# Weight parts made by two transfers and a ScalarE negation instead of a ScalarE copy and a VectorE subtraction

## The chip, the core and the metric

The kernel runs on one core of a Trainium2 chip. The metric is the device time of one execution in microseconds (us). The engines are named as the profile names them: PE is TensorE's matmuls, PEld its weight loads, DVE VectorE, ACT ScalarE, POOL GpSimd, SP the SyncE queue, which issues nearly every transfer of the kernel before.

## What is computed

The reference is one inference step of a two-layer network over 640 tokens (128 of context, 512 latent), with 1024 features, in float32. Each layer normalises its input, projects it with `w_in`, runs three token mixers beside each other (differential attention, a state-space scan, neighbourhood attention), merges them through gates, and projects with `w_out`:

```
def _pre(x, cvec, norm_g, w_ada, b_ada, w_in):
    ada = (jax.nn.silu(cvec) @ w_ada + b_ada)[..., None, :]
    shift, scale, gate = jnp.split(ada, 3, axis=-1)
    hmod = _rmsnorm(x, norm_g) * (1.0 + scale) + shift
    parts = jnp.split(hmod @ w_in, np.cumsum(IN_SIZES)[:-1].tolist(), axis=-1)
    return parts, gate

def _post(x, gate, ya, ga, yb, yc, gc, merge_logits, w_br_a, w_br_b, w_br_c, w_out):
    ma, mb, mc = jnp.split(jax.nn.sigmoid(merge_logits), N_BRANCH, axis=-1)
    merged = (ma * ((ya * jax.nn.silu(ga)) @ w_br_a) + mb * (yb @ w_br_b)
              + mc * ((yc * jax.nn.silu(gc)) @ w_br_c))
    return x + gate * (merged @ w_out)
```

The last layer is followed by one more normalisation. The matrices that the change touches are `w_in` (in the kernel `w_feat`, `w_v` and `w_z`, cut by use), the three `w_br` and `w_out`. `w_ada` goes another way.

## The kernel before, in words

**Exact pairs.** A float32 matrix product is made of three products in the type float32r, which keeps fewer bits. Every operand is held as a pair: `hi`, the value rounded to float32r, and `lo`, the rest. `feat` (L156) and `tok` (L173) multiply high by high, high by low and low by high into one PSUM bank. So each weight block must be in SBUF as two tiles before PE can use it: `lo` is wanted by the third product after the first use of `hi`.

**Where the pairs come from.** `weights` (L136) makes the pair of one block, a "set" in what follows. It is called 194 times: 12 sets of 256 KB (128 x 512) at the very start, 182 of 512 KB (8 of them 528 KB). SP loads the block into `raw`; ACT copies it into `hi`, which rounds (L144); DVE subtracts `hi` from `raw` into `lo` (L145). There are two `raw` tiles, three `hi` and three `lo`. A `raw` tile is free as soon as DVE has read it, so the next loads run while PE is still busy with older sets. A `hi` and a `lo` tile are free when PE has made its last product with them. The two `raw` tiles also take the blocks of `w_ada` that `ada_part` loads during neighbourhood attention.

**What a set feeds.** Most sets feed 48 products of 320 columns (`feat`, both halves of the tokens). The 12 sets at the start and the 32 of `w_out` feed 24 each, since `out_proj` loads each block once for each half of the tokens. `w_z` and `w_v` (8 sets each over both layers) are used two sets at a time by `tok`: five token tiles, each with 12 products of the first set and then 12 of the second.

**Order of the stages.** A start that loads x and the first adaLN blocks and works on the 12 small sets; then per layer the state-space branch with `w_z`, `w_v` and logits; differential attention; neighbourhood attention; and the tail, `merges` of the third branch and `out_proj` for each half. A scheduler in the framework sets the order of the instructions on each engine from the program and its own model of durations. At run time each engine takes its instructions strictly in that order, and each waits at its place. A transfer that POOL issues stands in POOL's order like its arithmetic. POOL in the kernel before makes products for the rotary embedding (L392) and the scan (L690, L735, L757), small powers for the norms (L191, L294) and fills padding (L573); it issues no transfer.

Of the kernel before, what the change touches and what calls it, by code (L numbers as in the profile page):

```python
# [19 lines left out]
EPS = 1e-6  # L20
# [11 lines left out]
# what fills the waits of each head (pair): logits of branches a and c, merges of branch a; and what stands before it  # L32
# [86 lines left out]
class Net:  # L119
# [15 lines left out]
    # ---- weights, each as an exact pair of float32r parts  # L135
    def weights(self, src, k, n):  # L136
        """[128, k, n] from DRAM -> its two parts."""
        nc = self.nc
        view = lambda t: t[:, 0:k * n].rearrange("p (k n) -> p k n", k=k)
        raw = view(self.wraw.tile([128, 1056], F32, tag="raw", name="raw"))  # L140
        self.dma(raw, src)
        hi = view(self.whi.tile([128, 1056], F32R, tag="hi", name="hi"))
        lo = view(self.wlo.tile([128, 1056], F32R, tag="lo", name="lo"))
        nc.scalar.activation(hi, raw, AF.Copy)  # L144
        nc.vector.tensor_tensor(out=lo, in0=raw, in1=hi, op=ALU.subtract)  # L145
        next(self.side, None)
        return hi, lo
# [10 lines left out]
    def feat(self, w, rhs, evac, m=0, halves=(0, 1), part=None):  # L158
        """128 output features of 640 tokens, handed to evac(half, PSUM [128, 320]); part: of a half of the rows alone."""
# [13 lines left out]
    def tok(self, w, t, n):  # L173
        """[128 tokens, n] of a token tile in PSUM."""
# [10 lines left out]
    def rstd(self, pool, ps, scale, n, eps_scale=1.0):  # L185
        """(ps * scale + EPS) ** -0.5 for a narrow [128, n]."""
# [12 lines left out]
    # ---- constants  # L199
# [33 lines left out]
    # ---- adaLN vectors: [128, feature tiles, 2 (context, latent)] each  # L233
    def ada_part(self, src, bias, dst, raws, p, pp):
        """1024 columns, side by side over the four column groups of the PE array; one step per 128 rows."""
# [18 lines left out]
    def ada(self, l, out, raws, p, pp):  # L254
        """Shift and scale, as (shift, (1 + scale) * norm_g) of four feature tiles each."""
# [20 lines left out]
    # ---- RMS of x over features, for one half of the tokens: PSUM [128, 320] of 1/rms on every partition  # L276
# [44 lines left out]
    def gate_in(self, l, c, p):  # L321
        """2 * silu of a gate tile."""
# [17 lines left out]
    # ---- differential attention  # L340
# [36 lines left out]
    def lat_part(self, half):  # L377
        """Where the latents of a half lie: in PSUM, among the latents."""
        return (slice(128, 320), slice(0, 192)) if half == 0 else (slice(0, 320), slice(192, 512))
# [43 lines left out]
    def diff_attn(self, l, h, v, kq, nlam, p, cp, ps, pp, after_ctx):  # L423
        """The head's output times the first map's normaliser, and that normaliser per token."""
# [8 lines left out]
        def soft(s, n, t):  # L433
            """exp(scale * (s - max)) of both maps, s [128, 2, n]; the first plus c times the second."""
# [15 lines left out]
        # context queries read context keys alone  # L450
# [13 lines left out]
        for qp in range(2):  # L464
            ph = p.tile([128, 6, 256], F32R, tag="ph", name="ph")
            pl = p.tile([128, 6, 256], F32R, tag="pl", name="pl")
            for qi in range(2):
# [12 lines left out]
                # the low parts of both maps side by side, each on its half of the rows and in its own bank  # L480
# [22 lines left out]
    def diff_norm(self, att, cp, pp):  # L503
        """Normaliser of the head's features per token, spread over the diagonals of a [128, 640]."""
# [13 lines left out]
        # rows of both parts of r, one token tile each  # L518
# [22 lines left out]
    # ---- state-space branch  # L541
    def ssd(self, l):
        nc, a, o, sm = self.nc, self.a, self.o, self.sm
        with ExitStack() as es:
# [97 lines left out]
            # softplus: max(x, 0) + log1p(exp(-|x|)), log1p(e) = 2 atanh(e / (2 + e))  # L642
# [26 lines left out]
            # decays: to the chunk's end (0, 1), from its start (2, 3), over all of it (4, 5); per direction  # L669
# [120 lines left out]
    # ---- neighbourhood attention: keys by blocks of eight columns (7, 0, 1, ..., 6), queries by tiles of sixteen columns  # L790
    def na_vkq(self, l, hp, p, pp, after_v=lambda: None):
# [17 lines left out]
        # values, token-major through transposes  # L809
# [26 lines left out]
        # keys  # L836
# [17 lines left out]
        # queries  # L854
# [22 lines left out]
    def na_ctx(self, vkq, y, p, ps, pp):  # L877
        """Context queries read context keys alone."""
# [77 lines left out]
    # ---- gated merge of one branch: twice its term, summed in DRAM or handed out  # L956
# [208 lines left out]
```

## Time and profile before

| | |
|---|---|
| median of the runs | 1662.32 us (2 runs, 1660.53 to 1664.1) |
| profiled execution, span | 1666.2 us |
| PE busy | 1601.4 us, 96% |
| DVE busy | 1062.0 us, 64% |
| ACT busy | 769.3 us, 46% |
| POOL busy | 149.8 us, 9% |
| transfers | 214.61 MB, 129 GB/s in the mean |

Matmuls are pipelined: each is shown for some 0.31 us, though one follows another every 0.14 us, so a busy PE can still be waiting a little. The page has the sums over the span; the trace behind it can be asked for one stretch, one engine or one line. In a row of the trace "idle before <-releaser" tells how long the engine stood still before the instruction and what ended that.

### The profile page before, as it was taken

The page shows a single profiled execution, that of the slowest core. Times are in us where ns is not written, and L with a number is a line of the kernel's source. Part 1 is how long each engine was busy: PE and PEld are TensorE (multiplying, and loading weights), DVE is VectorE, ACT ScalarE, POOL GpSimd, SP SyncE. Part 2 cuts the span into 40 slices and gives each one's busy share as a digit, 9 for nine tenths or more (in the row PEclk, how much of TensorE's full clock was granted, in tenths as well). Part 3 has the DMA queues.
Part 4 walks back from the last instruction along what each step waited for, and adds up shares of the span by engine and source line. Part 5 has one row for each costly group of instructions (what it writes and reads, how often), then busy time and mean ns, then how long its engine had stood idle before and what let it go on. Part 6 is the DMA issues. An engine that isn't in the chain of part 4 may idle for free.

```text
span 1666.2 us, 28800 instructions
## 1 busy us (share of the span) xinstructions
PE 1601.4 (96%) x11166; PEld 1495.2 (90%) x11166; DVE 1062.0 (64%) x2287; ACT 769.3 (46%) x1776; POOL 149.8 (9%) x170
## 2 busy tenths in 40 slices
PE   4999999999999999999999999999999999999997
PEld 2998898999888888889989989988998898999997
DVE  3886767657546465566688668756565374667566
ACT  3647633345444454443446565334444354554432
POOL 0005210101000000000000242201010000000000
PEclk9999999999999999999999999999999999999998
DMA  9422235322265755457542222352222946445553
GB/s 300 125 87 74 83 125 157 96 79 78 75 123 147 155 133 156 152 189 264 175 129 85 83 87 87 115 184 69 72 84 73 161 143 118 111 126 164 192 168 132
DMA packets 114824, 214.61 MB, mean 129 GB/s; under 512 B 36736, under 2 KB 52608, under 8 KB 114688
## 3 DMA queue, kind: packets, MB, share of 16 engines
q1 hardware_dynamic: 114688, 212.78, 44.2%
q8 instruction: 88, 1.44, 0.4%
q14 instruction: 48, 0.39, 0.1%
HBM read 170.27 MB, written 34.08 MB: 123 GB/s over the span
## 4 chain that ended last, share of the span: by engine, by line
PE 74%; DMA 12%; DVE 6%; ACT 3%; issue 3%; SPq 1%; POOL 1%; POOLq 0%; DVEq 0%; ACTq 0%
PE mm L170 51%; PE mm L182 7%; DMA raw<-in_w_feat 4%; DVE lo L145 2%; PE s L913 2%; PE t L929 1%; ACT hi L144 1%; DMA qd<-qr 1%; PE o L498 1%; PE o L937 1%; DMA aw<-in_w_ada 1%; PE g L740 1%; PE ada L242 1%; PE y L753 1%; PE t L490 1%
## 5 line engine op out<-in xcount | busy, mean ns | idle before, releaser
L170 PE MATMUL mm<-hh,hi 128*128 128x320 f32 x1856 | 581.0, 313 | 6.0 <-ACT hh L317 4.4
L170 PE MATMUL mm<-hl,hi 128*128 128x320 f32 x1856 | 580.4, 313 | 2.4 <-DVE hl L318 2.4
L170 PE MATMUL mm<-hh,lo 128*128 128x320 f32 x1856 | 576.7, 311 | 0.5 <-DVE lo L145 0.5
L170 PEld LDWEIGHTS mm<-hh,hi 128*128 128x128 f32 x1856 | 350.7, 189 | 25.8 <-issue 13.1
L170 PEld LDWEIGHTS mm<-hl,hi 128*128 128x128 f32 x1856 | 350.8, 189 | 10.4 <-issue 4.5
L170 PEld LDWEIGHTS mm<-hh,lo 128*128 128x128 f32 x1856 | 351.3, 189 | 6.3 <-issue 4.3
L145 DVE TENSOR_TENSOR lo<-raw,hi 128x1024 fp32r<-128x1024 f32 (+2 forms) x194 | 235.4, 1214 | 158.1 <-ACT hi L144 157.4
L144 ACT ACTIVATE hi<-raw 128x1024 fp32r<-128x1024 f32 (+2 forms) x194 | 200.0, 1032 | 246.7 <-PE mm L170 127.0
L170 PE MATMUL mm<-yh,hi 128*128 128x320 f32 x384 | 121.6, 318 | 8.8 <-DVE th L981 7.1
L170 PE MATMUL mm<-yl,hi 128*128 128x320 f32 x384 | 120.1, 313 | 0.2 <-DVE yl L338 0.2
L170 PE MATMUL mm<-yh,lo 128*128 128x320 f32 x384 | 119.3, 311 | 0.0
L182 PE MATMUL mm<-lo,hh 128*128 128x264 f32 (+1 forms) x320 | 90.7, 284 | 0.0
L182 PE MATMUL mm<-hi,hl 128*128 128x264 f32 (+1 forms) x320 | 90.7, 284 | 0.0
L182 PE MATMUL mm<-hi,hh 128*128 128x264 f32 (+1 forms) x320 | 90.2, 284 | 0.0
L170 PEld LDWEIGHTS mm<-yh,hi 128*128 128x128 f32 x384 | 72.7, 190 | 15.2 <-DVE th L981 9.3
L492 ACT ACTIVATE ph<-t 128x384 fp32r<-128x384 f32 x64 | 31.3, 489 | 113.3 <-PE t L490 113.3
L437 DVE TENSOR_REDUCE st<-s 128x2 f32<-128x1536 f32 (+1 forms) x40 | 59.5, 1487 | 30.4 <-PE s L483 25.8
L170 PE MATMUL mm<-mgh,lo 128*128 128x320 f32 x256 | 78.3, 308 | 0.4 <-DVE lo L145 0.4
L170 PE MATMUL mm<-mgl,hi 128*128 128x320 f32 x256 | 78.6, 308 | 0.0
L170 PE MATMUL mm<-mgh,hi 128*128 128x320 f32 x256 | 77.5, 306 | 0.0
L170 PEld LDWEIGHTS mm<-yl,hi 128*128 128x128 f32 x384 | 73.1, 190 | 0.6 <-DVE yl L338 0.4
L170 PEld LDWEIGHTS mm<-yh,lo 128*128 128x128 f32 x384 | 73.2, 191 | 0.0
(286 smaller groups left out, 2865.7 us busy)
## 6 DMA issues: line engine op xcount, KB each, us to landing
raw<-in_w_feat SPq DMA_DIRECT2D x110, 512.0 KB, 3.7
raw<-in_w_ada SPq DMA_DIRECT2D x32, 512.0 KB, 4.4
raw<-in_w_out SPq DMA_DIRECT2D x32, 512.0 KB, 3.9
thd<-th SPq DMA_DIRECT2D x48, 320.0 KB, 2.2
th<-thd SPq DMA_DIRECT2D x48, 320.0 KB, 3.8
raw<-in_w_br SPq DMA_DIRECT2D x24, 512.0 KB, 3.6
accd<-th SPq DMA_DIRECT2D x32, 320.0 KB, 3.5
ac<-accd SPq DMA_DIRECT2D x32, 320.0 KB, 4.5
```

The source lines that it names most:

```text
L144: nc.scalar.activation(hi, raw, AF.Copy)
L145: nc.vector.tensor_tensor(out=lo, in0=raw, in1=hi, op=ALU.subtract)
L170: nc.tensor.matmul(ps, lhsT=s, rhs=r, start=(k == 0 and n == 0), stop=(k == K - 1 and n == 2))
L182: nc.tensor.matmul(ps, lhsT=s, rhs=r, start=(k == 0 and q == 0), stop=(k == 7 and q == 2))
L242: nc.tensor.matmul(ps[32 * g:32 * g + 32, :], lhsT=self.sc[:, k, :], rhs=raw[:, 256 * g:256 * g + 256], start=(k == 0), stop=(k == 7))
L437: nc.vector.tensor_reduce(out=st[:, 0:2], in_=s, axis=AX.X, op=ALU.max)
L490: nc.tensor.transpose(pt[:, i, :], e[:, kt * 128:(kt + 1) * 128], self.ident)
L492: nc.scalar.activation(ph[dst], pt[:, 0:3, :], AF.Copy)
L498: nc.tensor.matmul(ov[:, 0:256], lhsT=x[:, kt, sv], rhs=q[:, kt, :], start=(kt == 0 and n == 0), stop=(kt == 5 and n == 2))
L740: nc.tensor.matmul(sg, lhsT=self.trir[:, d, :], rhs=rh.rearrange("p h n -> p (h n)"), start=(d == 0 and i == 0), stop=(d == 1 and i == 1))
L753: nc.tensor.matmul(yd[:, h * 64:h * 64 + 64], lhsT=ma[:, r], rhs=xt[:, c, h * 64:h * 64 + 64], start=True, stop=True)
L913: nc.tensor.matmul(s[:, c0:c0 + n], lhsT=q[:, i * 128:(i + 1) * 128], rhs=ks[j][:, k0:k0 + n], start=(x == 0), stop=(x == 1))
```

## The change

`weights` no longer loads `raw`. POOL issues a transfer from DRAM straight into the `hi` tile; since source and destination differ in type, the transfer rounds. ACT writes the negated `hi` into the `lo` tile. POOL then issues a second transfer of the same block into `lo` that adds to what is there. The VectorE subtraction is gone, and so is SP's part. The pools keep their sizes: three `hi`, three `lo`, two `raw`, which now serve `w_ada` alone. Everything else in the diff is removed comments and docstrings; by that, later lines move up by two.

```diff
     def weights(self, src, k, n):
-        """[128, k, n] from DRAM -> its two parts."""
-        nc = self.nc
+
         view = lambda t: t[:, 0:k * n].rearrange("p (k n) -> p k n", k=k)
-        raw = view(self.wraw.tile([128, 1056], F32, tag="raw", name="raw"))
-        self.dma(raw, src)
         hi = view(self.whi.tile([128, 1056], F32R, tag="hi", name="hi"))
         lo = view(self.wlo.tile([128, 1056], F32R, tag="lo", name="lo"))
-        nc.scalar.activation(hi, raw, AF.Copy)
-        nc.vector.tensor_tensor(out=lo, in0=raw, in1=hi, op=ALU.subtract)
+        self.nc.gpsimd.dma_start(out=hi, in_=src)
+        self.nc.scalar.activation(lo, hi, AF.Copy, scale=-1.0)
+        self.nc.gpsimd.dma_start(out=lo, in_=src, accum_op=ALU.add)
         next(self.side, None)
         return hi, lo
```

The order of the instructions changes with it. On POOL, late in the state-space branch of the first layer, where logits follow one another, the kernel before had only its own arithmetic (`rh` and `xw` are scan products, `rs` a power):

```order
L735 TENSOR_TENSOR rh<-masks,lh 128x512 x4
L757 TENSOR_TENSOR ysb<-xt,ds 128x512
L191 TENSOR_TENSOR rs<-rv,mhalf 128x1
L757 TENSOR_TENSOR ysb<-xt,ds 128x512
L191 TENSOR_TENSOR rs<-rv,mhalf 128x1
```

At the same place the change has (numbers tell the sets apart; `lo` is always one more than its `hi`):

```order
L141 DMA hi_2603<-in_w_feat 128x1024
L755 TENSOR_TENSOR ysb_1878<-xt_694,ds_692 128x512
L143 DMA lo_2604<-in_w_feat 128x1024
L141 DMA hi_2662<-in_w_feat 128x1024
L189 TENSOR_TENSOR rs_1896<-rv_1894,mhalf_116 128x1
L143 DMA lo_2663<-in_w_feat 128x1024
L755 TENSOR_TENSOR ysb_1992<-xt_694,ds_692 128x512
L141 DMA hi_2745<-in_w_feat 128x1024
L143 DMA lo_2746<-in_w_feat 128x1024
```

The two transfers of a set stand one behind the other, and the next set's first transfer stands behind the second of the set before; POOL's arithmetic stands between them.

In `out_proj` of the first layer the loads stood on SP, ahead of PE by as many as buffers allowed, mixed with stores of x (`xd`):

```order
L133 DMA raw_8970<-in_w_out 128x1024
L133 DMA raw_9003<-in_w_out 128x1024
L133 DMA xd_105<-x0_8855 128x320
L133 DMA xd_105<-x1_8856 128x320
L133 DMA raw_9036<-in_w_out 128x1024
L133 DMA raw_9069<-in_w_out 128x1024
```

Now they stand on POOL, three sets under way at a time:

```order
L141 DMA hi_8883<-in_w_out 128x1024
L141 DMA hi_8915<-in_w_out 128x1024
L143 DMA lo_8884<-in_w_out 128x1024
L141 DMA hi_8947<-in_w_out 128x1024
L143 DMA lo_8916<-in_w_out 128x1024
L143 DMA lo_8948<-in_w_out 128x1024
L141 DMA hi_8979<-in_w_out 128x1024
```

Here the first transfers of two further sets go ahead of the second transfer of the first one.

On ACT, among the logits of the same stretch as the first pair of fences, the kernel before had the rounding copy, with the evacuations of PSUM (`th`) around it:

```order
L962 ACTIVATE th_2447<-mm_2454 128x320
L144 ACTIVATE hi_2630<-raw_2628 128x1024
L962 ACTIVATE th_2447<-mm_2480 128x320
L743 ACTIVATE ee<-g 128x512
L787 ACTIVATE yh_97<-yf 128x128
```

and the change has the negation, which reads what the first transfer brings:

```order
L960 ACTIVATE th_2425<-mm_2457 128x320
L142 ACTIVATE lo_2604<-hi_2603 128x1024
L960 ACTIVATE th_2484<-mm_2490 128x320
L773 ACTIVATE ysq,yst<-ysb 128x512
L960 ACTIVATE th_2484<-mm_2516 128x320
```

The ACT instruction of a set keeps its place between two evacuations, but what it waits for is now a transfer that could not start before the buffer was free.

## Rows read from the trace of the kernel before

**Rows 1.** The page: span, then busy time of each engine.
```profile
span 1666.2 us, 28800 instructions
PE 1601.4 (96%) x11166; PEld 1495.2 (90%) x11166; DVE 1062.0 (64%) x2287; ACT 769.3 (46%) x1776; POOL 149.8 (9%) x170
```

**Rows 2.** PE's waits: for what, us in total, times, longest.
```profile
PE ada L242 <- DMA aw<-in_w_ada: 16.0, 5, 13.7
PE mm L170 <- DVE th L981: 7.1, 6, 2.8
...
PE mm L170 <- DVE hl L318: 2.4, 2, 1.8
...
PE mm L170 <- DVE lo L145: 1.0, 2, 0.5
```

**Rows 3.** Groups by line: busy us, mean ns | idle before, releasers.
```profile
L145 DVE TENSOR_TENSOR lo<-raw,hi 128x1024 fp32r<-128x1024 f32 (+2 forms) x194 | 235.4, 1214 | 158.1 <-ACT hi L144 157.4
L144 ACT ACTIVATE hi<-raw 128x1024 fp32r<-128x1024 f32 (+2 forms) x194 | 200.0, 1032 | 246.7 <-PE mm L170 127.0 <-DMA raw<-in_w_feat 72.3 <-DMA raw<-in_w_out 28.1
```

**Rows 4.** ACT's timeline among logits: start, us, instruction [idle before <-releaser].
```profile
227.27 1.06 ACT L144 ACTIVATE hi<-raw 128x1024 fp32r<-128x1024 f32 x1 [2.21 <-PE mm L170]
228.23 0.42 ACT L962 ACTIVATE th<-mm 128x320 f32<-128x320 f32 x1
...
234.67 1.06 ACT L144 ACTIVATE hi<-raw 128x1024 fp32r<-128x1024 f32 x1 [1.42 <-PE mm L170]
...
241.60 1.06 ACT L144 ACTIVATE hi<-raw 128x1024 fp32r<-128x1024 f32 x1 [1.29 <-PE mm L170]
```

**Rows 5.** Stretches: bounds, length, busy (count) by engine, PEclk, DMA share, GB/s.
```profile
0.00:45.00 45.00, 23.22 (x176) 11.95 (x177) 19.48 (x60) 15.97 (x37) 2.38 (x18) 0.92 0.91 292
45.00:83.00 38.00, 38.00 (x265) 38.00 (x265) 32.05 (x79) 21.69 (x44) 0.34 (x6) 1.00 0.38 120
500.00:780.00 280.00, 271.45 (x1933) 247.71 (x1932) 160.13 (x401) 125.03 (x318) 2.24 (x13) 1.00 0.59 164
805.00:851.00 46.00, 46.00 (x320) 45.84 (x319) 35.28 (x79) 23.67 (x41) 0.85 (x1) 1.00 0.62 192
1606.00:1653.00 47.00, 46.55 (x321) 46.13 (x320) 31.74 (x57) 17.83 (x26) 0.85 (x1) 1.00 0.47 152
1653.00:1666.20 13.20, 2.75 (x12) 1.50 (x10) 5.61 (x14) 0.47 (x1) 0.85 (x1) 0.61 0.29 99
```

**Rows 6.** ACT's timeline inside `out_proj` of the first layer.
```profile
814.96 1.06 ACT L144 ACTIVATE hi<-raw 128x1024 fp32r<-128x1024 f32 x1 [2.64 <-DMA raw<-in_w_out]
...
817.91 1.06 ACT L144 ACTIVATE hi<-raw 128x1024 fp32r<-128x1024 f32 x1 [1.54 <-DMA raw<-in_w_out]
```

**Rows 7.** ACT's timeline where one pair of `w_z` sets follows another.
```profile
97.16 1.09 ACT L144 ACTIVATE hi<-raw 128x1056 fp32r<-128x1056 f32 x1 [1.12 <-PE mm L182]
98.56 0.39 ACT L638 ACTIVATE sz<-mm 128x256 f32<-128x256 f32 x1 [0.32 <-PE mm L182]
```

**Rows 8.** PE's timeline in the same place: start, us, product.
```profile
96.31 0.28 PE L182 MATMUL mm<-lo,hh 128*128 128x264 f32 x1
96.42 0.28 PE L182 MATMUL mm<-hi,hl 128*128 128x264 f32 x1
```

**Rows 9.** Transfers: count, KB each, median us from issue to landing.
```profile
raw<-in_w_feat SPq DMA_DIRECT2D x110, 512.0 KB, 3.7
...
raw<-in_w_feat SPq DMA_DIRECT2D x12, 256.0 KB, 3.0
```

**Rows 10.** A POOL group by line: a power on three elements, busy us, mean ns.
```profile
L294 POOL TENSOR_TENSOR r<-v,mhalf 128x3 f32<-128x3 f32 x6 | 5.1, 850 | 440.1 <-DVE v L293 440.1
```

**Rows 11.** ACT's waits from 500 to 780 us: for what, us in total, times, longest.
```profile
ACT hi L144 <- DMA raw<-in_w_feat: 48.5, 17, 7.4
...
ACT hi L144 <- DMA raw<-in_w_br: 6.5, 3, 3.7
```

## The prediction

> **What bounds the kernel now.** I read the page first. PE is busy for 1601.4 of 1666.2 us, while DVE, from which the change takes work, is busy for 64% [rows 1]. So the question is not how much work DVE loses but whether PE waits for a weight set, now or afterwards. The second view is what PE waits for. `lo`, the result of the subtraction, costs PE 1.0 us in the whole execution; all that PE waits for DVE in the rows shown is 7.1 + 2.4 + 1.0 = 10.5 us [rows 2]. The 235.4 us of subtractions [rows 3] lie beside PE's work, and removing them can give back some 10 us at most. The third view is ACT's timeline: among logits each rounding copy starts when PE releases a `hi` buffer, at 227.27, 234.67 and 241.60 us [rows 4], with its `raw` block already in SBUF. That early load is what the change gives up.
>
> **How long a set takes, and how long it may.** After a buffer's release the old kernel needed 1.03 us on ACT and 1.21 on DVE [rows 3], 2.2 us. The new one needs, one after another: POOL's issue, the casting transfer, the negation, a second issue, the accumulating transfer. Nothing of this can start before the release, since the first transfer writes into `hi` itself. I call the sum L.
>
> The trace holds no POOL transfer, so each price is bounded. *Issue:* between nothing and some 0.85 us, which POOL takes for a power on three elements, where hardly any data is moved [rows 10]; I take 0.85. *Casting transfer:* 3.7 us as the plain load of the same block [rows 9], at worst twice that; I take 3.7. *Negation:* 1.03 us, the copy it replaces, of the same shape [rows 3]. *Accumulating transfer:* it must read the block and the tile that it adds to. In the first 45 us, with the transfer engines 91% busy, 292 GB/s were moved [rows 5], so 0.52 MB take 1.8 us of the 3.7 and 1.9 us are fixed; twice the bytes give 1.9 + 3.6 = 5.5. Bounds: 3.7 and 7.4. So L = 0.85 + 3.7 + 1.03 + 0.85 + 5.5 = 12 us, between 8.4 (both transfers plain, issues free) and 17.5 (all at their worst).
>
> The Trainium skill has prices for this, and they are lower: "DMA: Bandwidth & Descriptors" (Anatomy of one DMA, SWDGE path) fits a GpSimd transfer as 2.0 us plus its bytes at 436 GB/s, 3.2 us here, and "Collectives: The Full Stack" (The bandwidth ceiling) says that an add in the transfer engines moves at half the rate of a copy, because it reads two sources. By these, as an estimate, the accumulation would take 4.4 us, L would be 10.3, and the sum about 110 us in place of 142. No run here shows either figure, so the sum goes by the rows.
>
> With three buffers, a set written into a released buffer is wanted when the other two have been used up. I call that time R and compare it with L stage by stage.
>
> *Main stages (150 of the 194 sets).* R is two sets' products: 241.60 - 227.27 = 14.3 us among logits, the densest place [rows 4]; in attention other work lies between. L = 12 is hidden; at 17.5 it isn't.
>
> *Tail.* A `w_out` set feeds 24 products, at 46.0 / 320 = 0.144 us each [rows 5] 3.45 us, so R is 6.9. The old copies follow each other after 2.95 us [rows 6]; that stage just kept up. Each buffer now goes round in L + 3.45 us, and three do so together (the order on POOL allows it): one set per (12 + 3.45) / 3 = 5.15 us, 1.7 more than now. The two tail stretches of 46 and 47 us [rows 5] hold 27 sets; three more of layer 2's first projection use one half each: 30 x 1.7 = **51 us** (15 at L = 8.4, 106 at 17.5).
>
> *Start.* From 45 to 83 us the small sets follow each other in the same way [rows 5]. A 256 KB load lands in 3.0 us [rows 9]; L is 0.85 + 3.0 + 0.5 + 0.85 + 3.9 = 9.1, so 4.2 us per set, and nine sets wait: 9 x 0.7 = **7 us** (0 to 22).
>
> *Pairs of `tok`.* A pair holds two of the three buffers to its last token tile. The first set's `hi` is rewritten at 97.16 us, the pair's last bank is evacuated at 98.56 [rows 7], and the new set is wanted 12 products of 0.12 us later [rows 8], at 100.0: R = 2.9. Old parts needed about that. There are two such places in each layer (second `w_z` pair, `w_v` pair): 4 x (12 - 2.9) = **36 us** (22 to 58).
>
> *ACT's queue.* The negation keeps the copy's place and now waits there for the casting transfer; behind it stand evacuations and the exponentials and copies of attention, for which PE waits next. At most 150 x (0.85 + 3.7) = 683 us of waiting; ACT often comes later than the release, so I take half, 340. What this costs PE: from 500 to 780 us ACT waited 48.5 + 6.5 = 55 us for loads [rows 11] and PE lost 280 - 271.45 = 8.6 us for all reasons [rows 5], at most 0.155 for each us. So 340 x 0.155 = **53 us** (0 to 106). POOL's products, which now stand behind transfers, are taken as part of this.
>
> *Gain.* Half of the 10.5 us of waits for DVE: -5.
>
> Sum: 51 + 7 + 36 + 53 - 5 = 142 us on the profiled 1666.2: 1808. The profile was 3.9 us above the median of 1662.3, so I expect **1804 us**. The bounds of the terms give 15 + 0 + 22 + 0 - 10 = 27 and 106 + 22 + 58 + 106 = 292: 1689 and 1954.
>
> **Rivals.** *POOL's order becomes the bound.* In the main stages the next set's first transfer stands behind the second transfer of the set before, and that waits for the negation. So one set takes at least issue + cast + negation + issue: 6.4 us at my prices, under the 7.2 us at which logits follow each other [rows 4]. If the cast takes 7.4 us, it is 10.1, above it: 150 x 10.1 = 1515, 30 tail sets at (17.5 + 3.45) / 3 = 7.0 make 210, the start 83 + 22 = 105, and POOL's own 150 us [rows 1] stand in the same queue: 1980 us. For it: POOL really holds both transfers in line. Against it: nothing shows a cast to be slower than a copy. It decides from a cast of about 4.5 us on.
>
> *Everything stays hidden (not slower).* If L is at most R of the tail, 6.9 us, which needs both transfers to land within (6.9 - 1.03) / 2 = 2.9 us with free issues, only the pairs lose, 4 x 4 = 16 us, against up to 10 us won: 1662 + 6 = 1668, no change. The plain load's 3.7 us speaks against it. For faster by 2%, 33 us, PE would have to give back half of its 65 us of idle time [rows 1]; 21.8 of these are the start, before 45 us, and 10.5 the last norm [rows 5], and the change touches neither.
>
> *Only the stages without slack pay.* ACT's waits cost nothing, because the scheduler's order has work between: 1804 - 53 = 1751. It is my forecast with one term less, still slower.
>
> **How the numbers follow.** Chances: my forecast 0.45, the tail-and-pairs case 0.20 (together 1696 to 1900), POOL as the bound 0.20 (1900 to 2050), hidden 0.15. Of the last, 0.12 lie within 2% (33 us, about what a measurement of this kernel tells from no change) and 0.03 below. So slower 0.85, same 0.12, faster 0.03. The time is that of the forecast, 1804. The range has to reach into both outer cases: from 1665, just under the hidden case, to 1980, the POOL case; that leaves out some 0.06 below and 0.12 above.
>
> **What would show it.** In the changed profile DVE should lose about 235 us and ACT stay near 770. Right: POOL's first transfer of a set lands about 4.5 us after the release, the second 12 us after; PE's waits for `lo` rise from 1 us to some 90, nearly all in the tail, the start and the pairs; the stretch of `out_proj` in each layer grows by about 25 us. Wrong: a cast landing after 6 us or more and logits at over 9 us per set (then POOL bounds), PE idle in attention behind exponentials more than behind weights (then ACT's term is too small), or `out_proj` unchanged (then L is under 7). Most likely wrong: the accumulating transfer's price, which no row comes near.

## The result and the profile after

The changed kernel takes 1890.42 us (median of two runs, 1887.8 to 1893.05) against 1662.32: a ratio of 1.138, 95% interval 1.134 to 1.142. It is 14% slower. The forecast was 1804 us with a range of 1665 to 1980. The sign and the range held; the loss is 228 us where 142 were forecast.

The page of the changed kernel, its span, the busy times and the transfer queues (packets, MB, the time of their packets as a share of 16 engines), answers [rows 1]:

```profile
span 1891.3 us, 29037 instructions
PE 1682.4 (89%) x11166; PEld 1556.5 (82%) x11166; DVE 880.4 (47%) x2093; ACT 768.4 (41%) x1776; POOL 405.0 (21%) x558
...
q0 software_dynamic: 55872, 197.42, 48.7%
q1 hardware_dynamic: 86752, 114.07, 20.8%
```

VectorE's work went down as the change says and ACT's stayed (768.4 us). PE's idle time rose by 144 us, from 65 to 209, and its busy time by 81 us for the same 11166 products: together the 225 us by which the span grew. What PE waits for in the changed kernel (us, times, longest), beside [rows 2]:

```profile
PE mm L168 <- DMA lo<-in_w_out: 46.0, 18, 4.9
PE mm L168 <- DMA lo<-in_w_feat: 21.5, 9, 5.1
PE ms L290 <- DVE acc L284: 15.5, 2, 13.7
PE mm L168 <- DVE th L979: 14.8, 10, 3.7
PE mm L180 <- DMA lo<-in_w_z: 12.8, 4, 3.8
PE mm L180 <- DMA lo<-in_w_v: 11.3, 2, 6.3
PE mm L168 <- ACT th L960: 10.0, 5, 3.3
```

Waits for `lo` were 1.0 us before. They are now 46.0 + 21.5 + 12.8 + 11.3 = 91.6 us in the rows shown, the "some 90" of the forecast.

To see where the 228 us lie I cut both executions at the same products of PE: the first product with `w_z`, the first state product of the scan, the first of differential attention, of neighbourhood attention, the first and the last with `w_out`. The lengths in us:

| stage | before | after | longer by |
|---|---|---|---|
| start | 83.2 | 104.7 | 21.5 |
| `w_z` and `w_v` pairs, layers 1 and 2 | 50.7 + 50.8 | 66.1 + 59.9 | 24.5 |
| scan | 108.5 + 107.7 | 116.6 + 121.7 | 22.1 |
| differential attention | 259.6 + 261.8 | 275.2 + 277.1 | 31.0 |
| neighbourhood attention | 292.2 + 274.7 | 303.3 + 293.1 | 29.6 |
| `out_proj` | 57.0 + 57.8 | 101.2 + 96.8 | 83.2 |
| first projection of layer 2 | 49.6 | 62.6 | 13.0 |

The sum is 224.9 us. The scan and attention rows, "the six stretches" in what follows, make 82.7 of it. These stages don't hold quite the same work: the new order moves some 80 products from the `w_z` and `w_v` stages into the scan. PE's counts show it in those stages, before and after (bounds, length, busy times, PEclk, transfer share and GB/s):

```profile
83.20:133.80 50.60, 50.60 (x416) 49.76 (x414) 44.19 (x104) 28.32 (x67) 7.38 (x7) 1.00 0.23 72
900.70:951.50 50.80, 50.80 (x416) 49.93 (x414) 34.63 (x83) 25.12 (x59) 7.35 (x7) 1.00 0.20 61
...
104.70:170.80 66.10, 52.33 (x381) 50.59 (x379) 35.55 (x89) 25.96 (x61) 15.17 (x18) 0.90 0.49 103
1029.70:1089.70 60.00, 49.45 (x372) 48.10 (x370) 27.19 (x69) 21.78 (x54) 14.31 (x17) 0.91 0.48 100
```

At the pace of before (0.12 us a product in these rows) that is some 10 us. For the same work, then, the pairs lost about 35 us and the six stretches about 74.

**One set in `out_proj`.** POOL's, ACT's and PE's timelines in the first layer (start, us, instruction [idle before <-releaser]), in place of [rows 6]:

```profile
895.20 0.55 POOL L141 DMA_DIRECT2D hi<-in_w_out  x1 [1.88 <-PE mm L168]
...
901.00 0.88 POOL L143 DMA_DIRECT2D lo<-in_w_out  x1 [1.78 <-ACT lo L142]
...
899.64 1.06 ACT L142 ACTIVATE lo<-hi 128x1024 fp32r<-128x1024 f32 x1 [3.34 <-DMA hi<-in_w_out]
...
906.51 0.64 PE L168 MATMUL mm<-mgh,lo 128*128 128x320 f32 x1 [3.28 <-DMA lo<-in_w_out]
906.94 0.47 PE L168 MATMUL mm<-mgh,hi 128*128 128x320 f32 x1
907.21 0.47 PE L168 MATMUL mm<-mgl,hi 128*128 128x320 f32 x1
...
912.15 0.31 PE L168 MATMUL mm<-mgl,hi 128*128 128x320 f32 x1
912.30 0.31 PE L168 MATMUL mm<-mgh,lo 128*128 128x320 f32 x1
```

The buffer is released at 895.0 and POOL issues the cast 0.2 us later. `hi` has landed at 899.6; ACT negates; at 901.0 the accumulation is issued; at 906.5 `lo` has landed and PE goes on, after 3.28 us of waiting. That is 11.5 us for this set. The mean over the 31 `w_out` sets that can be followed is 13.6: 0.2 to the issue, 5.8 for the cast, 1.6 for the negation and the step to the next issue, 6.0 for the accumulation. The last rows show something that the forecast did not count: right after the wait one product follows another after 0.27 us, and from 911.4 us on after 0.145.

The granted clock tells why (length, busy times, PEclk, transfer share and GB/s of the two `out_proj` stretches):

```profile
865.90:967.10 101.20, 74.81 (x397) 71.27 (x396) 28.20 (x76) 29.39 (x49) 24.29 (x34) 0.80 0.83 192
1781.60:1878.30 96.70, 71.41 (x393) 68.07 (x392) 22.06 (x51) 21.94 (x30) 20.84 (x29) 0.84 0.73 166
```

In [rows 5] it was 1.00 there. A mean of 0.80 between 1.2 and 2.4 GHz says that TensorE ran at 1.2 GHz for 40% of the first stretch. Over the whole execution the mean is 0.946 (0.989 before): 204 us at 1.2 GHz against 37. That is where the 81 us of added busy time come from: 167 us more at 1.2 GHz, with products at nearly half the pace.

**ACT's place.** ACT's and PE's timelines in differential attention:

```profile
360.22 0.44 ACT L326 ACTIVATE gate<-mm 128x320 f32<-128x320 f32 x1
367.18 1.06 ACT L142 ACTIVATE lo<-hi 128x1024 fp32r<-128x1024 f32 x1 [6.53 <-DMA hi<-in_w_feat]
368.14 0.47 ACT L490 ACTIVATE ph<-t 128x384 fp32r<-128x384 f32 x1
...
366.55 0.31 PE L168 MATMUL mm<-hl,hi 128*128 128x320 f32 x1
368.67 0.39 PE L496 MATMUL o<-ph,vh 128*128 128x256 f32 x1 [1.81 <-ACT ph L490]
```

ACT stands for 6.5 us behind a cast, with the rounding `ph` queued behind the negation, and PE waits 1.8 us for `ph`. In the six stretches PE waits for ACT 41.5 us in all (14.7 before), for DVE 19.8 (7.9), for `lo` 7.6 (0).

The landing times (count, KB, median us from issue), beside [rows 9]:

```profile
hi<-in_w_feat POOLq DMA_DIRECT2D x110, 512.0 KB, 5.2
lo<-in_w_feat POOLq DMA_DIRECT2D x110, 512.0 KB, 5.6
...
hi<-in_w_out POOLq DMA_DIRECT2D x32, 512.0 KB, 6.2
lo<-in_w_out POOLq DMA_DIRECT2D x32, 512.0 KB, 5.4
```

The accumulation lands as forecast (5.5). The cast was priced at 3.7 and takes 5.2 to 6.2. Sorted by what is under way within the first 2.5 us of each cast, the medians are 4.0 us for 27 casts with neither beside them, 4.8 for 21 beside a transfer of SP, and 5.4 to 6.5 for 146 beside an accumulation.

### The profile page after: what moved, and what is told of

Its sections match the earlier page's. It is cut to its first block, busy times and chain, and to the rows that moved or that the text cites. A ratio compares the mean times of both kernels' runs of the same rounds, so it can differ in the third digit from the quotient of the medians.

```text
span 1891.3 us, 29037 instructions
## 1 busy us (share of the span) xinstructions
PE 1682.4 (89%) x11166; PEld 1556.5 (82%) x11166; DVE 880.4 (47%) x2093; ACT 768.4 (41%) x1776; POOL 405.0 (21%) x558
## 4 chain that ended last, share of the span: by engine, by line
issue 50%; PE 24%; DMA 12%; POOL 10%; DVE 2%; ACT 2%; POOLq 0%; SPq 0%; DVEq 0%; ACTq 0%
PE mm L168 14%; DMA hi<-in_w_feat 6%; POOL lo L143 5%; PE mm L180 3%; POOL hi L141 3%; PE g L738 1%; ACT lo L142 1%; PE o L496 1%; DMA raw<-in_w_ada 1%; DMA hi<-in_w_br 1%; PE y L751 1%; PE t L488 1%; DMA lo<-in_w_v 1%; DMA ac<-accd 1%; PE s L472 1%
## 5 line engine op out<-in xcount | busy, mean ns | idle before, releaser
L168 PE MATMUL mm<-hh,hi 128*128 128x320 f32 x1856 | 589.8, 318 | 16.4 <-ACT th L960 10.0
L168 PE MATMUL mm<-hh,lo 128*128 128x320 f32 x1856 | 584.0, 316 | 21.5 <-DMA lo<-in_w_feat 21.5
L142 ACT ACTIVATE lo<-hi 128x1024 fp32r<-128x1024 f32 (+2 forms) x194 | 200.5, 1033 | 479.5 <-DMA hi<-in_w_feat 258.7
L168 PEld LDWEIGHTS mm<-hh,lo 128*128 128x128 f32 x1856 | 358.1, 193 | 31.6 <-DMA lo<-in_w_feat 24.1
L143 POOL DMA_DIRECT2D lo<-in_w_feat x122 | 107.3, 880 | 612.8 <-ACT lo L142 515.2
L168 PE MATMUL mm<-mgh,lo 128*128 128x320 f32 x256 | 91.9, 362 | 46.0 <-DMA lo<-in_w_out 46.0
L141 POOL DMA_DIRECT2D hi<-in_w_feat x122 | 75.0, 615 | 263.8 <-PE mm L168 226.8
L180 PE MATMUL mm<-lo,hh 128*128 128x264 f32 (+1 forms) x320 | 95.8, 300 | 24.3 <-DMA lo<-in_w_z 12.8
L168 PEld LDWEIGHTS mm<-mgh,lo 128*128 128x128 f32 x256 | 57.7, 226 | 51.3 <-DMA lo<-in_w_out 51.1
L168 PE MATMUL mm<-mgh,hi 128*128 128x320 f32 x256 | 89.1, 351 | 4.7 <-DMA hi<-in_w_out 4.3
L168 PE MATMUL mm<-mgl,hi 128*128 128x320 f32 x256 | 88.8, 348 | 0.0
L491 DVE TENSOR_TENSOR pl<-t,ph 128x384 fp32r<-128x384 f32 x64 | 35.4, 553 | 113.2 <-ACT ph L490 113.0
L180 PEld LDWEIGHTS mm<-lo,hh 128*128 128x128 f32 x320 | 64.8, 203 | 25.9 <-DMA lo<-in_w_z 14.0
```

The costliest lines, as they stand in the source:

```text
L141: self.nc.gpsimd.dma_start(out=hi, in_=src)
L142: self.nc.scalar.activation(lo, hi, AF.Copy, scale=-1.0)
L143: self.nc.gpsimd.dma_start(out=lo, in_=src, accum_op=ALU.add)
L168: nc.tensor.matmul(ps, lhsT=s, rhs=r, start=(k == 0 and n == 0), stop=(k == K - 1 and n == 2))
L180: nc.tensor.matmul(ps, lhsT=s, rhs=r, start=(k == 0 and q == 0), stop=(k == 7 and q == 2))
L491: nc.vector.tensor_tensor(out=pl[dst], in0=pt[:, 0:3, :], in1=ph[dst], op=ALU.subtract)
```

## The experiments

Four theories share the loss. **A**: a set's time from release to landed `lo` against what three buffers cover. **B**: the transfer engines themselves are the limit. **C**: ACT, in its strict order, stands behind the cast. **D**: the traffic alone slows SP's transfers. The runs of before beside them had medians of 1659 to 1665 us. The table gives, against the kernel before, the ratio with its interval and the stages by the cut above, in us:

| kernel | us | ratio | start | pairs | six stretches | `out_proj` | layer 2 in |
|---|---|---|---|---|---|---|---|
| changed | 1890.4 | 1.138 (1.134 to 1.142) | 21.5 | 24.5 | 82.7 | 83.2 | 13.0 |
| e1, fourth pair | 1789.1 | 1.076 (1.073 to 1.080) | 7.9 | 0.2 | 63.4 | 44.0 | 7.0 |
| e2, cast only | 1725.5 | 1.037 (1.032 to 1.041) | 0.9 | 8.4 | 34.4 | 20.2 | 5.1 |
| e3, accumulation only | 1810.3 | 1.089 (1.086 to 1.092) | 12.5 | 25.5 | 51.8 | 44.1 | 8.4 |
| e4, `w_out` the old way | 1815.8 | 1.093 (1.089 to 1.096) | 22.0 | 24.3 | 85.7 | -0.8 | 14.9 |
| e5, zeros in `lo` | 1772.5 | 1.068 (1.066 to 1.069) | 10.3 | 10.5 | 26.9 | 51.8 | 7.0 |
| e6, negation on POOL | 2014.2 | 1.213 (1.209 to 1.218) | 26.3 | 40.4 | 134.2 | 125.1 | 16.6 |
| e7, filling products | 1893.8 | 1.141 (1.139 to 1.144) | 20.6 | 25.9 | 75.8 | 88.2 | 16.9 |
| e8, `w_out` alone the new way | 1755.7 | 1.058 (1.056 to 1.059) | -0.5 | 0.0 | -1.3 | 95.9 | -4.0 |
| e9, no accumulation | 1675.6 | 1.009 (1.007 to 1.011) | 0.7 | -2.1 | 6.4 | 4.1 | 2.0 |
| e10, traffic alone | 1666.9 | 1.005 (1.003 to 1.007) | 0.6 | 0.0 | -5.5 | 8.3 | -4.1 |
| e11, other order | 2126.4 | 1.278 (1.276 to 1.281) | 24.7 | 4.6 | 345.5 | 81.6 | 8.4 |
| e12, other order, no accumulation | 1821.4 | 1.097 (1.093 to 1.101) | 10.2 | -13.6 | 139.1 | 12.9 | 3.3 |

### A fourth pair of buffers

```
+        self.turn = (self.turn + 1) % 4
+        if self.turn == 3 and self.four:      # not in neighbourhood attention
+            hi, lo = (view(self.wraw.tile([128, 1056], F32R, tag="raw", name=n)) for n in ("hi", "lo"))
+        else: ...                              # hi and lo from their own pools, as before
```

> The changed kernel with a fourth pair of buffers: outside neighbourhood attention the two raw tiles, which are idle there, serve as a hi and a lo for every fourth set. Theory A (time from release to landed lo, 13 us in out_proj, against the time that the other buffers cover): a buffer goes round in 13 + 3.45 us and four do so together, 4.1 us per set in place of 5.6 to 6.0, so out_proj of the first layer takes about 75 us in place of 101 and that of the second about 70 in place of 97; the granted clock there goes back above 0.9, pairs and start gain some 15 us; total 1800 to 1825. Theory B (the transfers themselves are the limit, since two per set share POOL's queue): casts and accumulations get longer in step, out_proj stays above 95 us in each layer, total above 1870.

1789.1 us, 11 below the range of A and far from B. The two `out_proj` stretches (same columns as above):

```profile
831.80:909.30 77.50, 62.89 (x395) 60.01 (x394) 28.31 (x77) 28.38 (x48) 22.93 (x33) 0.96 0.99 238
1694.90:1776.00 81.10, 63.02 (x393) 59.75 (x391) 22.89 (x54) 22.16 (x31) 20.26 (x28) 0.96 0.83 194
```

A holds: one more buffer takes 101 us to 77.5 and 97 to 81, brings the clock back to 0.96, and the pairs lose nothing any more. But B has a part in what comes next: the transfer engines are 99% and 83% busy and casts and accumulations of `w_out` land after 7.4 and 7.3 us in the median, so a set comes every 4.8 to 5.1 us and not every 4.1. The six stretches gain only 19 of 83 us, 7 of them because less work was moved into the scan. Neighbourhood attention has no fourth pair, but differential attention has one and still loses 24 of its 31 us, so there the number of buffers is not what costs.

### One transfer at a time

```
 e2:  SP loads raw;  self.nc.gpsimd.dma_start(out=hi, in_=src)
                     self.nc.vector.tensor_tensor(out=lo, in0=raw, in1=hi, op=ALU.subtract)
 e3:  SP loads raw;  self.nc.scalar.activation(hi, raw, AF.Copy)
                     self.nc.scalar.activation(lo, hi, AF.Copy, scale=-1.0)
                     self.nc.gpsimd.dma_start(out=lo, in_=src, accum_op=ALU.add)
```

> Half of the change: SP loads raw early as before, POOL's casting transfer makes hi, VectorE subtracts hi from raw into lo; no negation, no accumulation. Theory A: from release to lo 0.55 + 4.3 + 1.2 = 6 us, under the 6.9 us that two w_out sets cover: out_proj near 58 us, PE waits for lo under 15 us, pairs lose 4 x 3 = 12 us; total 1675 to 1700. Theory C (what costs is that an engine stands in its order behind a transfer, now VectorE, with everything behind it late): the main stages keep most of their 80 us: 1730 to 1770, with PE waiting for VectorE's results.

> The other half: SP loads raw early, ScalarE rounds raw into hi as before and then writes the negated hi into lo, POOL's accumulating transfer adds the source. ScalarE has 194 operations more (some 200 us busy more). Theory A: from release to lo 1.03 + 1.03 + 0.9 + 5.5 = 8.5 us; out_proj (8.5 + 3.45) / 3 = 4.0 us per set, some 66 us per layer; pairs lose 4 x 5.6 = 22 us; total 1700 to 1730. Theory C: ScalarE no longer waits for a transfer that started late, so the main stages are back at the old lengths; they stay long only if ScalarE's added work costs PE something.

e2 came out at 1725.5, in neither range: between A (1675 to 1700) and C (1730 to 1770). e3 came out at 1810.3, 80 us above what I expected. In e3 ACT stands behind no transfer of POOL, and still the six stretches are 51.8 us longer; so ACT's place (C) isn't needed for a loss there. Each kernel moves every block twice, and their pages price the two kinds of transfer (queue of POOL: packets, MB, share of 16 engines' span; spans 1734.6 and 1808.9 us):

```profile
q0 software_dynamic: 27936, 98.71, 20.6%
```

```profile
q0 software_dynamic: 27936, 98.71, 31.4%
```

0.206 x 16 x 1734.6 / 98.71 = 57.9 us of one engine per MB for a cast, 0.314 x 16 x 1808.9 / 98.71 = 92.1 for an accumulation; SP's plain transfers of before, loads and stores together, took 0.442 x 16 x 1666.2 / 212.78 = 55.4 (its page: 212.78 MB, 44.2%). So a cast costs the engines about what a plain transfer does, and an accumulation 1.6 times as much. Cast and accumulation of one 0.524 MB block occupy all 16 engines for 0.524 x 150.0 / 16 = 4.9 us. By this estimate that is a floor under the pace of `out_proj` for any number of buffers, above the 3.45 us in which PE uses a set. e1's first stretch, 99% busy, stands at it; its second, 83% busy at 5.1 us, does not, and what holds that one was not tried. In e3 a plain load and an accumulation make 4.8 us, and its `out_proj` ran at 80.7 / 16 = 5.0.

### Only `w_out` the old way, only `w_out` the new way

```
 e4:  self.weights(a["w_out"][l, m], 8, 128, old=True)    # raw, copy, subtraction; all other sets: the change
 e8:  the reverse: w_out by the change, all other sets by raw, copy, subtraction
```

> The changed kernel, with the 32 sets of w_out made the old way (SP, ScalarE, VectorE), all others the new way. If the loss is local to the stages, the two out_proj stretches return to about 58 us, which gives 44 + 39 = 83 us: total near 1805. If the delay is passed on (the sets after out_proj now late instead), less than 60 us come back: above 1830.

> The kernel before with the 32 sets of w_out alone made the new way. If the loss of out_proj is local (chain against three buffers), the two stretches are as in the changed kernel, 97 to 101 us, and the other stages as before: 1663 + 83 = 1746, 1735 to 1755. If half of it came from other sets' transfers beside it or from a late start, out_proj takes under 85 us: below 1725.

Both local. In e4 the stretches are back to their old length to 1 us (two stretches, same columns), and nothing else moved:

```profile
868.50:925.50 57.00, 57.00 (x396) 56.84 (x394) 42.22 (x89) 27.34 (x47) 2.90 (x4) 1.00 0.57 185
1742.50:1799.50 57.00, 56.96 (x393) 56.53 (x392) 37.42 (x66) 21.50 (x30) 0.88 (x1) 1.00 0.39 135
```

e8 pays 41 + 55 us in `out_proj` and nothing elsewhere: 1755.7 us, just above the range. (Some 7 us of the 41 are 48 products of layer 2's first projection that its order puts inside this stretch; so that stage is shorter.) The losses add up but for some 11 us: +146 us in e4's stages and +90 in e8's make 236, against 225 in the changed kernel.

One thing in e8 was not expected: its second stretch takes 112.7 us, where the changed kernel has 96.8. There POOL's order puts the next set's cast ahead of a set's accumulation. ACT ended a negation at 1683.39 us, but POOL stood at the next cast until PE released that buffer, and the accumulation went out 3.8 us later, right behind it:

```profile
1686.62 0.55 POOL L147 DMA_DIRECT2D hi<-in_w_out  x1 [8.02 <-PE mm L174]
1687.15 0.91 POOL L149 DMA_DIRECT2D lo<-in_w_out  x1
```

Six of that layer's 16 sets waited 1.2 to 4.0 us in this way. In the first layer none did. So chain against buffers sizes the stage only where POOL's order lets each transfer go at once.

### The two transfers without the chain between them

```
-        self.nc.scalar.activation(lo, hi, AF.Copy, scale=-1.0)
+        self.nc.vector.memset(lo.bitcast(F32), 0.0)
```

> The changed kernel with the same two transfers per set, but VectorE writes zeros into lo where ScalarE wrote the negated hi; so lo holds the source itself (the rest is not made), and neither the second transfer nor any engine's order waits for the first. Theory A with C (what costs is the chain cast, negation, accumulation, and ScalarE standing behind the cast): from release to lo about 0.5 + 0.9 + 6 to 7 = 8 us, out_proj about 3.8 us per set, 62 to 68 us per layer, and differential and neighbourhood attention within 5 us of the kernel before; total 1690 to 1725. Theory D (the doubled traffic slows SP's own transfers and the engines that wait for them): these four stages stay 10 us or more longer each, total above 1750.

1772.5 us: D's total, but the four attention stretches are 3.0 to 9.8 us longer, neither all within 5 us nor 10 or more. The six stretches fall from +82.7 to +26.9, so two thirds of that loss hang on the chain (the accumulation and ACT both waiting for the cast). `out_proj` stays at +51.8: the two transfers of a set now run side by side, an accumulation of `w_out` lands after 7.8 us in the median, and the transfer engines are 89% and 90% busy, near the floor (5.6 and 4.8 us per set).

### The negation on GpSimd

```
-        self.nc.scalar.activation(lo, hi, AF.Copy, scale=-1.0)
+        self.nc.gpsimd.tensor_scalar(out=lo, in0=hi, scalar1=-1.0, scalar2=None, op0=ALU.mult)
```

> The changed kernel with the negation on GpSimd, so that neither ScalarE nor VectorE stands behind a transfer; the chain gets longer (by the 128x320 products of 0.8 to 1.07 us a negation takes some 2.5 us there, 1.5 more than on ScalarE) and POOL's order tighter. Theory C: the two stretches of differential attention come back to within 5 us of before (from +15.5), PE's waits for ScalarE's ph, e and qh back to the few us of before; out_proj 5 us longer per layer by the longer chain. Theory D: no stretch gets shorter. If POOL's order now bounds (0.6 + 5 + 2.5 + 0.9 = 9 us per set against 7.2), the logits of the scan stretches grow by some 10 us each. Total 1860 to 1930.

2014.2 us, 80 above the range. The group of the negation on POOL, and PE's largest wait:

```profile
L142 POOL TENSOR_SCALAR lo<-hi 128x1024 fp32r<-128x1024 f32 (+2 forms) x194 | 537.7, 2772 | 662.6 <-issue 208.6 <-DMA hi<-in_w_feat 190.3 <-PE mm L168 66.2
```

```profile
PE mm L168 <- DMA lo<-in_w_feat: 52.2, 28, 6.0
```

PE's waits for `ph`, `e` and `qh` did shrink to 0.8, 2.2 and none, as C has it, but attention did not come back: POOL now holds issue, cast, negation (2.77 us) and second issue of a set in line, with the next set's cast among them, and 73 of the 194 accumulations were issued more than 1 us after their negation, against 10 in the changed kernel. So I read it as the rival that the forecast had at 1980 us, made to happen. As a test of C it is inconclusive.

### Products that keep TensorE's clock up

```
+            fill = self.bank()[:, 0:320]
+            for k in range(12):
+                nc.tensor.matmul(fill, lhsT=mg[k % 8][0][:, 0:128], rhs=mg[k % 8][0][:, 0:320], start=True, stop=True)
```

> The changed kernel with 12 added products behind each w_out set, of operands that are in SBUF anyway, into a bank that nobody reads: PE does 384 products more (1.7 us per set at 0.144 us each) in time in which it waited. If the granted clock falls because PE waits, and the slow products then cost time, the clock in the two out_proj stretches rises from 0.80 and 0.84 to above 0.95, sets follow each other in (12.9 + 3.45) / 3 = 5.4 us, the stretches shrink from 101 and 97 to some 93 and 90, and the total falls by 10 to 20 us although PE does more: 1870 to 1880. If the clock has no part in it, the total stays or grows: 1890 or more.

```profile
870.00:972.20 102.20, 89.18 (x575) 86.65 (x574) 28.45 (x76) 27.81 (x47) 23.19 (x33) 0.97 0.79 184
1780.10:1880.90 100.80, 87.71 (x576) 85.20 (x575) 22.19 (x51) 21.95 (x30) 21.01 (x29) 0.98 0.69 160
```

The clock went up as expected (0.97 and 0.98), the time did not go down: 1893.8 us, and stretches of 102 and 101. PE made 45% more products in the same time. So filling the waits is no cure here. It looks as if the 1.7 us of added products per set ate what the clock gave back, but what the clock alone costs in `out_proj` this run can't separate.

### No accumulation, and traffic alone

```
 e9:  the change without   self.nc.gpsimd.dma_start(out=lo, in_=src, accum_op=ALU.add)
 e10: the kernel before with   nc.gpsimd.dma_start(out=self.spill[i], in_=hi)   behind the subtraction
```

> The changed kernel without the second transfer; lo stays the negated hi (the source is not added). ScalarE still stands behind the casting transfer, but the transfer engines have no more bytes to move than in the kernel before. From release to lo 0.55 + 4.5 + 1.03 = 6.1 us, so out_proj is back near 58 us and the pairs lose 4 x 3 = 12 us. Theory C (ScalarE's order behind the cast): differential and neighbourhood attention keep about 8 to 12 us of their +11 to +18 each; total 1710 to 1735. Theory D (the doubled traffic): they come back to within 3 us; total 1675 to 1690.

> The kernel before with one more transfer per set that nobody waits for: as soon as hi is written, POOL stores it to DRAM, into one of eight scratch places that nobody reads. So the transfer engines move as many bytes as in the changed kernel, while no set is ready later. Theory D: the stretches of attention grow by 5 to 10 us each, as SP's own loads and stores land later, total 1685 to 1710. If traffic alone costs nothing: 1660 to 1672. The hi buffer is held until the store has read it, which can make out_proj some us longer.

e9 is the sharpest result of the study: 1675.6 us, 0.9% above before. ACT's waits in the whole execution of e9 (us, times, longest):

```profile
ACT lo L142 <- DMA hi<-in_w_feat: 242.2, 98, 8.1
...
ACT lo L142 <- DMA hi<-in_w_out: 55.2, 27, 5.2
...
ACT lo L142 <- DMA hi<-in_w_br: 39.1, 18, 4.8
```

ACT stands 336.5 us behind casts, and PE loses next to nothing by it: the six stretches are 6 us longer, the total is what D expected. C alone falls. The pairs lost nothing where 12 us were expected.

e10 moves as many bytes as the changed kernel and reaches 1666.9 us: D by bytes falls too. D by the time of the transfer engines does not. e10's stores took 0.168 x 16 x 1665.5 / 98.71 = 45 us of one engine per MB, half of an accumulation's 92, and SP's own stores show the difference. Landing of the stores of `th` (count, KB, median us) before, in e10, in the changed kernel and in e3:

```profile
thd<-th SPq DMA_DIRECT2D x48, 320.0 KB, 2.2
...
thd<-th SPq DMA_DIRECT2D x48, 320.0 KB, 2.2
...
thd<-th SPq DMA_DIRECT2D x48, 320.0 KB, 5.0
...
thd<-th SPq DMA_DIRECT2D x48, 320.0 KB, 4.6
```

In e3, where ACT waits for no cast, PE waits 28.4 us in the six stretches for the `th` that DVE makes (7.0 before), and DVE waits 62 us for `th` to be loaded again (16 before). In e2, without accumulations, the stores take 4.7 us too. So slower transfers of SP look like a second way from the added transfers to PE; no run tests it alone.

### The same order with and without the accumulation

```
-    with tile.TileContext(nc, schedule_with_timeline_sim=True) as tc:
+    with tile.TileContext(nc, schedule_with_timeline_sim=False) as tc:
```

> The changed kernel, ordered by the framework's scheduler with its other model of durations. This run and the next one have nearly the same order on every engine (PE's instructions stand 1.1 places apart in the mean, ScalarE's 0.5), while the changed kernel and the one without the accumulation, as ordered so far, differ more. Compared with the next run. Theory O (the scan and attention stretches got longer because the scheduler arranged them differently around the late sets): with the same order, the six stretches together are less than 25 us longer here than in the next run (76 us in the pair ordered as before), and the whole some 150 us. Theory R (run time: with accumulations under way casts land later and sets are late, whatever the order): 60 us or more in the six stretches, some 210 us in all.

> The kernel without the accumulation (lo stays the negated hi) under the same other model of durations: the base for the run above. How long it is in itself tells nothing on the theories; by the order it may be some per cent longer than 1676 us. Its out_proj should take 56 to 62 us per layer, as with the order before.

The last question was whether the six stretches got longer because the scheduler laid them out differently. With nearly the same order the accumulation costs 345.5 - 139.1 = 206 us in them and 305 in all. So theory R holds: it acts at run time, and a changed order isn't needed. ACT's largest wait in each, e11 and then e12:

```profile
ACT lo L142 <- DMA hi<-in_w_feat: 430.6, 100, 10.7
```

```profile
ACT lo L142 <- DMA hi<-in_w_feat: 319.5, 99, 8.2
```

As many waits are a third longer where accumulations run. How much of it PE feels differs with the order: 206 us in this one, 82.7 - 6.4 = 76 in the kernel's own, of which some 6 are again work moved into the scan. That this order leaves less between a result and its use is my reading; no run tests it.

## Why the prediction was right, and where it was off

| term | forecast | stages longer by | of that, PE idle |
|---|---|---|---|
| tail (with layer 2's first projection) | 51 | 83.2 + 13.0 = 96 | 60.5 |
| start | 7 | 21.5 | 12.5 |
| pairs | 36 | 24.5 | 24.3 |
| ACT's queue, POOL's products | 53 | 82.7 | 46.5 |
| gain | -5 | not visible | |
| sum | 142 | 225 | 144 |

**Right, with luck: the waiting. Missing: the clock.** The forecast's terms are waits of PE, and as waits they came to 144 us against 142. That the sums meet is partly luck, since tail and start were too small and pairs and ACT's queue too large. What the forecast put at nothing is that TensorE's clock falls around such waits: the same products then kept PE busy 81 us longer. The forecast took the clock for given at 1.00, from [rows 5]. The two columns are an account, not a promise: with a full clock a part of the 81 us could turn into waiting, as e7 suggests, whose clock was 0.97 in `out_proj` and whose stretches were no shorter.

**Right: what bounds the kernel.** Taking 235 us from DVE bought nothing, and the early load of `raw` was what counted. e1 and e4 show the tail's mechanism as the forecast put it, chain against buffers; e8 adds POOL's order in one layer.

**Right as prices: negation and accumulation.** The accumulation, named as the most likely error, landed after 5.5 us as forecast. The Trainium skill's half rate for an add, which the page has for ring collectives ("Collectives: The Full Stack", The bandwidth ceiling), gave an estimate of 4.4 us; the runs differ, since by engine time the accumulation moves at 57.9 / 92.1 = 0.63 of a cast's rate and lands later than the estimate.

**Mis-sized: the cast.** 3.7 us by the plain load; alone it takes 4.0, and in the kernel it is rarely alone, since an accumulation of another set is mostly under way. The bound "twice that" held for the medians (5.2 to 6.2). The Trainium skill's fit for a GpSimd transfer ("DMA: Bandwidth & Descriptors", Anatomy of one DMA, SWDGE path) gave an estimate of 3.2 us, below every median here.

**Mis-sized: the tail.** With 13.6 us to landed `lo` the forecast's own formula gives (13.6 + 3.45) / 3 = 5.7 us per set; measured are 101.2 / 16 = 6.3 and 96.8 / 16 = 6.05. By these figures the missing part is the clock: from the landing to the end of a set that it waited for PE needs some 5 us instead of 3.45, because a part of its products run at 1.2 GHz. (13.6 + 5.0) / 3 = 6.2. No run separates this part.

**Mis-sized: the start.** The small sets needed 9.7 us from release to `lo` (forecast 9.1), for which the formula gives some 8 us; PE waited 12.5 us more there, and the granted clock of the stage was 0.89 in place of 0.96. e1 brings it from +21.5 to +7.9, so most is again the number of buffers. The 13.7 us for the norm's sums (`acc`) in the list of waits above are no loss: PE's first product starts at 13.7 us in both kernels, before it was one of `w_ada` [rows 2].

**Right in size, by another sum: the pairs.** Four places, as forecast, with 24.1 us of waits for `lo` of `w_z` and `w_v` in place of 36; they covered more of the chain than the 2.9 us that the forecast took from one place. The lower clock there (0.90 and 0.91) brings the loss to about 35 us for the same work.

**Near in the sum, wrong in the working: ACT's queue.** The forecast took 340 us of waits; in the six stretches ACT was idle for 356 us ahead of the negations. But a fixed rate of 0.155 us of PE per us of ACT doesn't fit: in e9 280 such us cost some 6, in the changed kernel 76 more of them came with 76 us of stage. Waits of over 4 us number 38 in the changed kernel and 18 in e9, so it looks as if short ones are covered by the order and long ones are not; that is a reading, not a test. One of the forecast's signs of being wrong came true: in the six stretches PE waits longer for ACT (41.5 us) than for weights (7.6), which it gave as the sign that ACT's term was too small.

What is shown is that neither ACT's wait (e9) nor as many bytes (e10) cost this alone, that the accumulation brings it at run time (e11 against e12), and that two thirds go when the chain is cut (e5). Of the 74 us for the same work 46.5 are waits of PE (27 more for ACT, 12 for DVE, 8 for `lo`), the rest goes with the lower clock. How far ACT's and DVE's results come late through late casts, and how far through slower transfers of SP, stays open.

**Rival "POOL's order".** Its condition, a cast above 4.5 us, was met, and still POOL did not bind: for 160 of 191 sets the cast was issued within 0.5 us of the release, and of the 132 sets of the six stretches 124 had landed before PE wanted them. The rival counted 7.2 us per set for every stage, but only the densest logits need that pace. It took e6's negation on POOL to make it true, and in e8 the order of one layer.

**Wrong as a sign to look for:** "DVE should lose about 235 us". It lost 181.6 busy us; the last section shows a part of the rest.

No kernel of the study beats the one before; the nearest that makes both parts of all sets in a new way, e2, is 3.7% slower.

## What to carry to other kernels

A transfer that writes straight into the tile which the consumer holds can't start before the release; a load into a staging tile can. Before moving arithmetic into transfers, add up the whole chain from release to ready and divide by the buffers, and then add up the engines' time per byte, because a second transfer of a block, and above all an accumulating one, sets a floor that more buffers don't lower. Relief for an engine that nobody waits for was worth nothing here. A sum of waits is not yet the loss: here 144 us of waiting came with 81 us of slower products behind the waits. And a wait on an engine's order can't be priced by its length times a mean rate: 280 us of ACT's waits cost 6 us in one kernel, 356 came with 83 in another.

## What the hardware showed that I had not expected

- An accumulating transfer occupies the transfer engines 1.6 times as long per byte as a casting or a plain one (92.1, 57.9 and 55.4 us of one engine per MB), and a cast lands after 4.0 us alone and 5.4 to 6.5 beside an accumulation.
- In the changed kernel TensorE was granted 1.2 GHz for 204 us, in `out_proj` around PE's waits of 3 to 5 us: a product then followed the last after 0.27 us in place of 0.145.
- VectorE's additions with both inputs in SBUF stretch when a product of POOL runs beside them. DVE's and POOL's timelines in the rotary embedding of the changed kernel:

```profile
289.04 1.61 DVE L391 TENSOR_TENSOR qr<-qr,sh 128x192 f32<-128x192 f32 x1 [0.17 <-POOL sh L390]
...
299.67 0.36 DVE L391 TENSOR_TENSOR kr<-kr,sh 128x192 f32<-128x192 f32 x1 [0.49 <-POOL sh L390]
...
288.74 0.78 POOL L141 DMA_DIRECT2D hi<-in_w_br  x1
289.35 1.07 POOL L390 TENSOR_TENSOR sh<-sh,rope 128x320 f32<-128x320 f32 x1
```

The same addition takes 0.36 us at 299.67, while POOL only issues a transfer (from 299.59 on), and 1.61 beside a POOL product. Four of its 16 instances take 1.61 to 2.29 us, each beside such a product, the others 0.36 at most; before all took 0.36 at most. The Trainium skill has this rule ("SBUF — State Buffer", Who interferes with whom): a VectorE instruction with two SBUF inputs and a GpSimd instruction that reads SBUF exclude each other on a shared port. The rows agree with it in effect. Nothing waited for VectorE long enough here for it to matter.
- Negating 128x1024 takes 2.77 us on POOL and 1.03 on ACT.
